# Summing the later modulation vectors over weight blocks on DVE, ACT and POOL in place of thin float32 matmuls

## Chip, core and metric

One core of a Trainium2 chip runs the whole kernel as one program. The metric is the device time of one execution in microseconds; the median of several runs is compared. TensorE does the matmuls, VectorE (DVE), ScalarE (ACT) and GpSimd (POOL) work on tiles in SBUF, and SyncE (SP) issues all the DMAs of this kernel.

## What is computed

Two layers of a diffusion backbone over 512 latent and 256 context tokens, model width 1024. In each layer the tokens are normalised and modulated, go through three groups of attention heads (neighbourhood, latent, differential), are gated, projected and added back. The change concerns the modulation vectors. For each layer and for each of two streams (latent: `c`, context: `c_ctx`) they come from one vector times a 1024 x 3072 matrix:

```python
shift, scale, gate = jnp.split(jax.nn.silu(c) @ w_ada[l] + b_ada[l], 3, axis=-1)
shift_c, scale_c, gate_c = jnp.split(jax.nn.silu(c_ctx) @ w_ada[l] + b_ada[l], 3, axis=-1)
h = rms_norm(x, norm_g[l]) * (1.0 + scale[:, None]) + shift[:, None]
hc = rms_norm(ctx, norm_g[l]) * (1.0 + scale_c) + shift_c
...
x_new = x + gate[:, None] * merge_branches(o_na, o_mla, o_diff, z, gm, w_br[l], w_out[l])
if not last:
    ctx = ctx + gate_c * merge_branches(co_na, co_mla, co_diff, cz, cgm, w_br[l], w_out[l])
```

The last layer needs the gate of the latent stream alone.

## The kernel before, in words

Activations lie transposed in SBUF as pairs of float32r tiles (a high part and what it leaves), so that each product is three matmuls (`mm3`, L115 to L117). Weights come in blocks of 128 x 384 by DMA (`unit`, tile `ws`, L138), ACT makes the high part (`w`, L122), DVE or POOL the low one (L127). A layer is a loop of twelve steps, each with the projection of one head pair (PSUM tiles `pj`, three banks), the attention of the pair before (`sc`, `bk`), a z gate and some gate projections (`zgate`, `gm`, PSUM tile `fl`, one bank); then come the branch projections and `out_proj`, which multiplies by `gate` (L1037).

The order of the instructions on each engine is not the order of the code. A scheduler goes through the program with priorities that the code sets per kind of work (`PRI`, `SHIFT`, `at`), takes what its own time model calls ready, and writes one fixed list per engine. On the chip each engine then takes its list strictly in order and waits where an operand is not there; SP's list of DMAs likewise.

`w_ada` is cut into 6 chunks per layer of 512 columns, each of 8 blocks of 128 x 512 (256 KB). Chunks 0 and 1 are the shift, 2 and 3 the scale, 4 and 5 the gate. The first four chunks of layer 0 are made in the setup (`fast`, tile `fs`) and are not touched. The eight later ones, (0,4), (0,5), all six of layer 1, are made by `ada_later` as background work of low priority (`ada` 2500). There, each block lands in one of four `aw` tiles, and a float32 matmul with the 128 x 32 tile `sT` (two columns of it are the two streams' vectors, the rest zero) adds it into one of four 32-row groups of the bank `fl` (L230). Each such matmul stands in the trace as two records. When eight blocks are in, DVE copies the bank to SBUF (`arow`, L231). For shift and scale, four small matmuls with the selector `C_SEL` (L250) add the row groups and turn the rows into columns, and DVE adds the bias (L254). For the gate, eight rows go to DRAM; `ada_gate` reads them back with the bias as a ninth row (L266, L267), and a matmul with `selb` (L270) sums them and spreads them over 128 partitions.

`rstd` (L166 on DVE, a power on POOL at L167) makes the norms' factors. `mla_prep` makes the latent head group's projections of all tokens at the start of each layer: projection into `pj`, square on ACT, `rstd`, a scaled copy `cn` on DVE, transposes on TensorE (L567), and split copies `ct` which go to DRAM.

Of the kernel before, what the change touches and what calls it, by code (L numbers as in the profile page):

```python
# [7 lines left out]
F32 = mybir.dt.float32  # L8
F32R = mybir.dt.float32r
AF = mybir.ActivationFunctionType  # L10
ALU = mybir.AluOpType
# [3 lines left out]
P = 128  # L15
D = 1024
KT = 8
# [19 lines left out]
C_SEL = 256  # L37
# [15 lines left out]
class Mixer:  # L53
# [114 lines left out]

    # ---------------------------------------------------------------- setup
    def setup(self):  # L170
# [44 lines left out]
    def ada_rows(self, l, ch, rows, pool, fast):  # L215
        nc, io = self.nc, self.io
        ps = self.fl()
        w = io["w_ada"][l, ch]
        for k in range(KT):
            if fast:  # L220
                st = pool.tile([P, 512], F32, tag="fs", bufs=self.FS, name=self.n("fs"))
            else:
                st = self.wpool.tile([P, 512], F32, tag="aw", bufs=4, name=self.n("aw"))
            if self.AFT and not fast:
                with self.tc.issue_after(self.last.ins):
                    nc.sync.dma_start(st, w[:, k])
            else:
                nc.sync.dma_start(st, w[:, k])
            g = 32 * (k % 4)
            nc.tensor.matmul(ps[g:g + 32, :], self.sT[:, k, :], st, start=k < 4, stop=k >= 4, tile_position=(0, g))  # L230
        nc.vector.tensor_copy(rows, ps)  # L231

    def ada_later(self, l, ch, pool):
        rows = pool.tile([P, 512], F32, tag="th", bufs=1, name=self.n("arow"))
        self.ada_rows(l, ch, rows, None, False)
        if ch < 4:
            self.ada_ss(l, ch, rows, self.fl())
            return
        if l not in self.rowsd:
            self.rowsd[l] = self.dram.tile([2, 4, 2, 512], F32, name=f"rowsd{l}")  # L240
        for g in range(4):
            self.nc.sync.dma_start(self.rowsd[l][ch - 4, g], rows[32 * g:32 * g + 2, :])

    def ada_ss(self, l, ch, rows, pt):
        nc = self.nc
        Lp = self.L[l]
        part, hf = ch // 2, ch % 2
        sel = self.cst[:, C_SEL:C_SEL + 2]
        for i in range(4):
            nc.tensor.matmul(pt[:, 2 * i:2 * i + 2], rows[:, i * P:(i + 1) * P], sel, start=True, stop=True)  # L250
        v = pt[:, 0:8].rearrange("p (k s) -> p k s", s=2)
        col = lambda o: Lp["pp"][:, o + 4 * hf:o + 4 * hf + 4].unsqueeze(2).to_broadcast([P, 4, 2])
        d = Lp["AB"[1 - part]][:, 4 * hf:4 * hf + 4, :]
        nc.vector.tensor_tensor(d, v, col(PP_BA + 8 * part), ALU.add)  # L254
        if part == 1:
            nc.vector.scalar_tensor_tensor(d, d, 1.0, col(PP_NG), ALU.add, ALU.mult)

    def ada_gate(self, l, pool):
        nc = self.nc
        strs = (0, 1) if l == 0 else (0,)  # L260
        gate = [pool.tile([P, D], F32, tag=f"gate{s}", bufs=1, name=f"gate{l}_{s}") for s in strs]
        selb = pool.tile([9, 2, P], F32, tag="selb", bufs=1, name=f"selb{l}")
        nc.sync.dma_start(selb, self.io["selb"])
        for hf in range(2):
            rows = pool.tile([9, 512], F32, tag="arow", bufs=1, name=self.n("arow"))
            nc.sync.dma_start(rows[0:8, :], self.rowsd[l][hf].rearrange("g s n -> (g s) n"))  # L266
            nc.sync.dma_start(rows[8:9, :], self.io["b_gate"][l:l + 1, hf * 512:(hf + 1) * 512])  # L267
            for s in strs:
                ps = self.bk()
                nc.tensor.matmul(ps, selb[:, s, :], rows[0:9, :], start=True, stop=True)  # L270
                nc.scalar.mul(gate[s][:, hf * 512:(hf + 1) * 512], ps, 0.25)
        return gate
# [34 lines left out]

    # ---------------------------------------------------------------- h
    def norm_tile(self, pool, xt):
# [66 lines left out]

    # ---------------------------------------------------------------- projections
    def proj_tok(self, ps, ws, t):
# [714 lines left out]
def _consts(np):  # L1093
    c = np.zeros((P, C_N), np.float32)
    c[:, C_ID:C_ID + P] = np.eye(P)
    c[:, C_ONE:C_ONE + P] = 1.0
    selb = np.zeros((9, 2, P), np.float32)
    selb[8] = 1.0
    for s in range(2):
        c[s::32, C_SEL + s] = 1.0  # L1100
        selb[s:8:2, s] = 1.0
    rope = np.zeros((P, S_N), np.float32)
    t = np.arange(SEQ)
    row, col = (t % 8).astype(np.float32), (t // 8).astype(np.float32)
    for co, so, dim in ((S_COSD, S_SIND, 64), (S_COSM, S_SINM, 32)):
# [7 lines left out]
    return c, selb, rope  # L1113


def _layout(np, i):
    a = {k: np.asarray(v) for k, v in i.items()}
    o = {}
    o["cst"], o["selb"], o["rope"] = _consts(np)
    o["x"] = a["x"][0].reshape(8, 64, D).transpose(1, 0, 2).reshape(SEQ, D)  # L1120
# [5 lines left out]
    w = kp(a["w_in"])  # L1126
# [41 lines left out]
```

## Time and profile before

| | |
|---|---|
| runs | 2012.0, 2018.39, 2019.07 us, median 2018.39 |
| profiled execution | span 2015.7 us from first to last instruction; no time beside the span is given for it |
| busy | TensorE 1962.4 us, DVE 1217.9, ACT 938.1, POOL 762.3 |
| granted TensorE clock, mean | 0.990 of full speed |

Span and busy times are of one execution under the hardware profiler. A busy TensorE is not one at its peak, since matmuls overlap and their ends are modelled; idle time before an instruction is put down to the engine or DMA whose signal came last.

### The profile page before, as it was taken

To read this page: it belongs to the slowest core of one execution; us is meant where nothing else is said; L and a number is where in the kernel's file an instruction comes from. 1 tells how busy PE (TensorE), PEld (TensorE's weight loads), DVE (VectorE), ACT (ScalarE), POOL (GpSimd) and SP (SyncE) were. 2 spreads that over 40 slices of the span, in tenths; PEclk is the share of its full clock that TensorE was granted. 3 is DMA by queue.
4 is the path that set the end of the run, shared out by engine and by line. 5 is a ranking of instruction groups with operands and counts; after the bars stand their busy time and mean duration, and the time that the engine had idled before them with its cause. 6 is when DMAs were issued, how large, how long until landed. Compare 5 with 4: busy or idle time off the path is not lost.

```text
span 2015.7 us, 33972 instructions
## 1 busy us (share of the span) xinstructions
PE 1962.4 (97%) x11650; PEld 1745.5 (87%) x11650; DVE 1217.9 (60%) x2808; ACT 938.1 (47%) x2422; POOL 762.3 (38%) x1053
## 2 busy tenths in 40 slices
PE   6999999999999999999999999999999999999998
PEld 4988998998888988989999988897698789889878
DVE  5556667555765555646663465667667466666763
ACT  4445455444544544435532354555455345555531
POOL 3333233323423322332355454334344234343353
PEclk9999999999999999999999999999999899999999
DMA  9553113333434333332655243323513322432663
GB/s 320 185 157 123 41 56 104 110 120 111 124 110 145 90 100 119 98 108 70 199 175 178 92 129 125 110 66 91 163 54 93 112 72 81 119 126 59 189 188 112
DMA packets 172600, 243.28 MB, mean 121 GB/s; under 512 B 22710, under 2 KB 127560, under 8 KB 172428
## 3 DMA queue, kind: packets, MB, share of 16 engines
q1 hardware_dynamic: 172428, 241.12, 38.3%
q8 instruction: 92, 1.51, 0.3%
q14 instruction: 80, 0.66, 0.1%
HBM read 190.38 MB, written 44.49 MB: 117 GB/s over the span
## 4 chain that ended last, share of the span: by engine, by line
PE 90%; DVE 4%; DMA 2%; ACT 1%; issue 1%; POOL 1%; SPq 0%; DVEq 0%; ACTq 0%; POOLq 0%
PE pj L115 11%; PE pj L117 11%; PE pj L116 11%; PE fl L115 10%; PE fl L116 9%; PE fl L117 9%; PE sc L690 9%; PE bk L851 5%; PE bk L680 4%; PE fl L230 2%; PE sc L731 2%; PE bk L810 2%; PE pj L640 1%; PE pj L451 1%; DVE w L127 1%
## 5 line engine op out<-in xcount | busy, mean ns | idle before, releaser
L122 ACT CAST w<-ws 128x384 fp32r<-128x384 f32 (+3 forms) x520 | 237.2, 474 | 268.4 <-PE fl L116 159.2
L127 POOL TENSOR_TENSOR w<-ws,w 128x384 fp32r<-128x384 f32 (+3 forms) x260 | 241.9, 936 | 312.6 <-ACT w L122 301.7
L115 PE MATMUL fl<-h,w 128*128 128x384 f32 (+1 forms) x864 | 316.5, 366 | 4.1 <-DVE zs L392 2.7
L115 PE MATMUL pj<-w,h 128*128 128x384 f32 (+2 forms) x944 | 314.5, 336 | 2.0 <-DVE kl L127 1.1
L117 PE MATMUL fl<-h,w 128*128 128x384 f32 (+1 forms) x864 | 312.8, 362 | 0.0
L116 PE MATMUL fl<-h,w 128*128 128x384 f32 (+1 forms) x864 | 312.8, 362 | 0.0
L116 PE MATMUL pj<-w,h 128*128 128x384 f32 (+2 forms) x944 | 309.6, 330 | 0.0
L117 PE MATMUL pj<-w,h 128*128 128x384 f32 (+2 forms) x944 | 307.5, 330 | 1.0 <-POOL h L127 0.6
L127 DVE TENSOR_TENSOR w<-ws,w 128x384 fp32r<-128x384 f32 (+2 forms) x260 | 177.4, 686 | 74.4 <-ACT w L122 67.0
L167 POOL TENSOR_TENSOR ss<-ss,nhalf 128x4 f32<-128x4 f32 (+1 forms) x144 | 142.8, 992 | 179.2 <-DVE ss L166 166.3
L694 ACT ACTIVATE P<-sc,st 128x768 f32<-128x768 f32 (+1 forms) x192 | 159.5, 832 | 104.7 <-DVE st L796 39.1
L741 POOL TENSOR_SCALAR P<-P,st 128x512 f32<-128x512 f32 (+1 forms) x128 | 107.8, 845 | 256.0 <-DVE st L737 216.7
L684 DVE TENSOR_TENSOR pt<-bk,pt 128x512 fp32r<-128x512 f32 (+1 forms) x256 | 147.8, 586 | 64.9 <-ACT pt L683 62.7
L117 PEld LDWEIGHTS pj<-w,h 128*128 128x128 f32 x944 | 177.0, 189 | 9.6 <-issue 5.9
L115 PEld LDWEIGHTS pj<-w,h 128*128 128x128 f32 x944 | 177.6, 189 | 8.8 <-issue 3.8
L116 PEld LDWEIGHTS pj<-w,h 128*128 128x128 f32 x944 | 178.2, 189 | 5.7 <-issue 5.0
L115 PEld LDWEIGHTS fl<-h,w 128*128 128x128 f32 x864 | 164.4, 190 | 18.3 <-DVE zs L392 4.9
L117 PEld LDWEIGHTS fl<-h,w 128*128 128x128 f32 x864 | 164.1, 190 | 13.1 <-DVE w L127 0.5
L683 ACT CAST pt<-bk 128x512 fp32r<-128x512 f32 (+1 forms) x256 | 126.9, 506 | 104.3 <-PE bk L680 101.8
L116 PEld LDWEIGHTS fl<-h,w 128*128 128x128 f32 x864 | 164.2, 190 | 11.0
L690 PE MATMUL sc<-qk,qk 96*128 96x512 f32 (+3 forms) x592 | 153.2, 353 | 3.0 <-DMA qk<-qk 3.0
L680 PE MATMUL bk<-cst,P 128*128 128x128 f32 x832 | 130.1, 274 | 2.7 <-DVE u L855 1.8
(236 smaller groups left out, 3995.9 us busy)
## 6 DMA issues: line engine op xcount, KB each, us to landing
ws<-in_w_qkv SPq DMA_DIRECT2D x128, 192.0 KB
ws<-in_w_gm SPq DMA_DIRECT2D x96, 192.0 KB
aw<-in_w_ada SPq DMA_DIRECT2D x64, 256.0 KB
ct<-cqd SPq DMA_DIRECT2D x40, 384.0 KB
ct<-ckd SPq DMA_DIRECT2D x48, 256.0 KB
ws<-in_w_z SPq DMA_DIRECT2D x48, 192.0 KB
thd<-th SPq DMA_DIRECT2D x48, 192.0 KB
ws<-in_w_br SPq DMA_DIRECT2D x48, 192.0 KB
```

The source lines that it names most:

```text
L115: mm(out, a[0], b[0], start=first, stop=False)
L116: mm(out, a[0], b[1], start=False, stop=False)
L117: mm(out, a[1], b[0], start=False, stop=last)
L122: nc.scalar.copy(hi, src)
L127: (nc.gpsimd if le == "g" else nc.vector).tensor_tensor(lo, src, f(hi), ALU.subtract)
L167: nc.gpsimd.tensor_tensor(out, out, self.nhalf[:, :cols], ALU.pow)
L680: nc.tensor.transpose(pt[:, i * P:(i + 1) * P], src[:, (b0 + i) * P:(b0 + i + 1) * P], self.ident)
L683: nc.scalar.copy(h, v)
L684: nc.vector.tensor_tensor(lo, v, f(h), ALU.subtract)
L690: mm(s[:, d0:d0 + w], x, y, start=i == 0, stop=i == len(ops) - 1)
L694: nc.scalar.activation(p, src, AF.Exp, bias=st[:, m:m + 1], accum_out=st[:, 2 + m:3 + m])
L741: nc.gpsimd.tensor_scalar(p, p, st[:, 4 + m:5 + m], 0.0, ALU.mult, ALU.add)
```

## The change

`ada_later` no longer uses TensorE for the blocks. Each chunk has an accumulator `acc` of 128 x 512 per stream in SBUF (one buffer). For the first block ACT writes block times the vector's entry of each partition; for the others DVE multiplies and adds for the latent stream, and for the context stream, where it is needed (six of the eight chunks), ACT multiplies the block in place and POOL adds it. What is left to do is a sum over the 128 partitions. For shift and scale, matmuls of `acc` slices with a column of ones do it, one for each stream and slice (eight in place of four). For the gate the whole accumulator goes to DRAM (256 KB per stream in place of 4 KB a row group), is read back by `ada_gate` one stream at a time, DVE adds the bias into its first row, and a matmul with the 128 x 128 ones sums and spreads it. The `aw` tiles are two in place of four.

```diff
     def ada_later(self, l, ch, pool):
-        rows = pool.tile([P, 512], F32, tag="th", bufs=1, name=self.n("arow"))
-        self.ada_rows(l, ch, rows, None, False)
+        nc = self.nc
+        strs = (0, 1) if l == 0 or ch < 4 else (0,)
+        acc = pool.tile([P, 2, 512], F32, tag="acc", bufs=1, name=self.n("acc"))
+        w = self.io["w_ada"][l, ch]
+        for k in range(KT):
+            st = self.wpool.tile([P, 512], F32, tag="aw", bufs=2, name=self.n("aw"))
+            nc.sync.dma_start(st, w[:, k])
+            for s in strs:
+                g = self.sT[:, k, s:s + 1]
+                if k == 0:
+                    nc.scalar.mul(acc[:, s], st, g)
+                elif s == 0:
+                    nc.vector.scalar_tensor_tensor(acc[:, s], st, g, acc[:, s], ALU.mult, ALU.add)
+                else:
+                    nc.scalar.mul(st, st, g)
+                    nc.gpsimd.tensor_tensor(acc[:, s], acc[:, s], st, ALU.add)
         if ch < 4:
-            self.ada_ss(l, ch, rows, self.fl())
+            pt = self.fl()
+            for i in range(4):
+                for s in strs:
+                    nc.tensor.matmul(pt[:, 2 * i + s:2 * i + s + 1], acc[:, s, i * P:(i + 1) * P], self.ones[:, 0:1], start=True, stop=True)
+            self.ada_put(l, ch, pt)
             return
         if l not in self.rowsd:
-            self.rowsd[l] = self.dram.tile([2, 4, 2, 512], F32, name=f"rowsd{l}")
-        for g in range(4):
-            self.nc.sync.dma_start(self.rowsd[l][ch - 4, g], rows[32 * g:32 * g + 2, :])
+            self.rowsd[l] = self.dram.tile([2, 2, P, 512], F32, name=f"rowsd{l}")
+        for s in strs:
+            nc.sync.dma_start(self.rowsd[l][ch - 4, s], acc[:, s])
...
         for hf in range(2):
-            rows = pool.tile([9, 512], F32, tag="arow", bufs=1, name=self.n("arow"))
-            nc.sync.dma_start(rows[0:8, :], self.rowsd[l][hf].rearrange("g s n -> (g s) n"))
-            nc.sync.dma_start(rows[8:9, :], self.io["b_gate"][l:l + 1, hf * 512:(hf + 1) * 512])
+            bias = pool.tile([1, 512], F32, tag="gbias", bufs=1, name=self.n("gbias"))
+            nc.sync.dma_start(bias, self.io["b_gate"][l:l + 1, hf * 512:(hf + 1) * 512])
             for s in strs:
+                rows = pool.tile([P, 512], F32, tag="arow", bufs=1, name=self.n("arow"))
+                nc.sync.dma_start(rows, self.rowsd[l][hf, s])
+                nc.vector.tensor_tensor(rows[0:1, :], rows[0:1, :], bias, ALU.add)
                 ps = self.bk()
-                nc.tensor.matmul(ps, selb[:, s, :], rows[0:9, :], start=True, stop=True)
+                nc.tensor.matmul(ps, self.ones, rows, start=True, stop=True)
                 nc.scalar.mul(gate[s][:, hf * 512:(hf + 1) * 512], ps, 0.25)
```

In the changed kernel most lines of the rest have numbers 17 higher (L680 is L697, L851 is L868); L115 to L167 keep theirs. The blocks' first products are L240, DVE's multiply-adds L242, ACT's products L244, POOL's adds L245.

The scheduler's lists move with it. On TensorE, these rows stood before at the last chunk of `ada_later`, in layer 1, at 1556 to 1566 us of the profile. `pj` is a projection of the latent heads, `fl` with L230 the chunk, `bk` with L680 transposes of probabilities, with L851 attention times V:

```order
L116 MATMUL pj_18796<-w_18787,ct_18797 128x256
L117 MATMUL pj_18796<-w_18786,ct_18797 128x256
L230 MATMUL fl_18512<-aw_18513,sT 32x512
...
L230 MATMUL fl_18512<-aw_18522,sT 32x512
L680 MATMUL bk_18041<-cst,P_18037 128x128 x4
L680 MATMUL bk_18052<-cst,P_18048 128x128 x4
L230 MATMUL fl_18512<-aw_18525,sT 32x512
L851 MATMUL bk_18059<-pt_17987,V_17582 128x256
```

And these stand there now, from the same projection to the same transposes (`fl` with L115 to L117 is a gate projection):

```order
L116 MATMUL pj_18884<-w_18875,ct_18885 128x256
L117 MATMUL pj_18884<-w_18874,ct_18885 128x256
L115 MATMUL fl_19153<-h_0_12883,w_19136 128x512
...
L116 MATMUL fl_19153<-h_1_12884,w_19148 128x512
L697 MATMUL bk_18134<-cst,P_18130 128x128 x4
L697 MATMUL bk_18145<-cst,P_18141 128x128 x4
L117 MATMUL fl_19153<-h_0_12883,w_19149 128x512
```

The chunk is gone from this place (it now lies at the start of the layer), and twenty matmuls of a gate projection, which stood behind it because they need the same bank, have moved ahead of the transposes.

On POOL, this is a piece of the difference at 54 to 69 us, in the context projections of `mla_prep` (`mss` are their norms' powers, `acc` the first chunk's adds for the context stream):

```order
 L167 TENSOR_TENSOR mss_654<-mss_654,nhalf 128x1
+L245 TENSOR_TENSOR acc_5052<-acc_5052,aw_5057 128x512
 L167 TENSOR_TENSOR mss_698<-mss_698,nhalf 128x1
+L245 TENSOR_TENSOR acc_5052<-acc_5052,aw_5062 128x512
+L245 TENSOR_TENSOR acc_5052<-acc_5052,aw_5067 128x512
 L167 TENSOR_TENSOR mss_742<-mss_742,nhalf 128x1
 L127 TENSOR_TENSOR w_815<-ws_811,w_814 128x384
```

The adds have come in between the powers; in the first 165 us there are 21 of them.

On DVE, these rows now stand in `mla_prep` of layer 1, from 1188 us of the profile before (`aw` numbers name the blocks of one chunk in turn; `cn`, `mss` and `ct` belong to the projections of the context and latent tokens):

```order
L242 SCALAR_TENSOR_TENSOR acc_17311<-aw_17321,sT,acc_17311 128x512
L576 TENSOR_SCALAR cn_14120<-pj_14095,mss_14121 128x384
L242 SCALAR_TENSOR_TENSOR acc_17311<-aw_17324,sT,acc_17311 128x512
L242 SCALAR_TENSOR_TENSOR acc_17311<-aw_17327,sT,acc_17311 128x512
L166 TENSOR_SCALAR mss_14160<-mss_14160 128x1
L588 TENSOR_TENSOR ct_14043<-bk_14040,ct_14043 128x256
L242 SCALAR_TENSOR_TENSOR acc_17311<-aw_17330,sT,acc_17311 128x512
L576 TENSOR_SCALAR cn_14159<-pj_14134,mss_14160 128x384
```

Before, none of the L242 rows were there; the chunk ran at 1439 to 1450 us on TensorE. Block 17327 takes the buffer of block 17321, two blocks before it.

## Rows read from the trace of the kernel before

**Rows 1.** The page: span; busy by engine; GB/s by slice; the ending chain.

```profile
span 2015.7 us, 33972 instructions
...
PE 1962.4 (97%) x11650; PEld 1745.5 (87%) x11650; DVE 1217.9 (60%) x2808; ACT 938.1 (47%) x2422; POOL 762.3 (38%) x1053
...
GB/s 320 185 157 123 41 56 104 110 120 111 124 110 145 90 100 119 98 108 70 199 175 178 92 129 125 110 66 91 163 54 93 112 72 81 119 126 59 189 188 112
...
PE 90%; DVE 4%; DMA 2%; ACT 1%; issue 1%; POOL 1%; SPq 0%; DVEq 0%; ACTq 0%; POOLq 0%
PE pj L115 11%; PE pj L117 11%; PE pj L116 11%; PE fl L115 10%; PE fl L116 9%; PE fl L117 9%; PE sc L690 9%; PE bk L851 5%; PE bk L680 4%; PE fl L230 2%; PE sc L731 2%; PE bk L810 2%; PE pj L640 1%; PE pj L451 1%; DVE w L127 1%
```

**Rows 2.** Timeline of TensorE, first chunk: start, length (us), instructions.

```profile
439.54 1.06 PE L230 MATMUL fl<-aw,sT 128*32 128x512 f32 x8
...
448.05 0.34 PE L116 MATMUL pj<-w,h 128*128 128x384 f32 x1
448.32 1.05 PE L230 MATMUL fl<-aw,sT 128*32 128x512 f32 x4
449.30 0.44 PE L117 MATMUL pj<-w,h 128*128 128x384 f32 x1
```

**Rows 3.** Groups by line and shape, whole span: busy, mean ns, idle before.

```profile
L230 PE MATMUL fl<-aw,sT 128*32 128x512 f32 x128 | 39.2, 626 | 4.6 <-DMA aw<-in_w_ada 3.7 <-ACT th L990 0.9
```

**Rows 4.** Timeline of TensorE in the last chunk, and a window with its clock.

```profile
1563.34 1.05 PE L230 MATMUL fl<-aw,sT 128*32 128x512 f32 x2 [3.70 <-DMA aw<-in_w_ada]
...
1567.02 1.92 PE L230 MATMUL fl<-aw,sT 128*32 128x512 f32 x2
...
1577.67 0.63 PE L115 MATMUL fl<-h,w 128*128 128x512 f32 x1
...
1564.00:1582.00 18.00, 18.00 (x55) 11.83 (x55) 3.94 (x9) 2.93 (x8) 0.92 (x2) 0.53 0.12 40
```

**Rows 5.** Groups by line: L250 from 600 to 1000 us, L270 whole span.

```profile
L250 PE MATMUL fl<-cst,arow 128*128 128x2 f32 x32 | 3.8, 240 | 0.0
...
L270 PE MATMUL bk<-arow,selb 9*128 9x512 f32 x12 | 6.5, 631 | 1.2 <-DMA arow<-rowsd 1.2
```

**Rows 6.** Timeline at the end: the last gate rows.

```profile
1963.01 0.29 SPq L266 DMA_DIRECT2D arow<-rowsd  x1
...
1969.46 1.12 PE L270 MATMUL bk<-arow,selb 9*128 9x512 f32 x2 [1.22 <-DMA arow<-rowsd]
```

**Rows 7.** Groups by line and shape: instructions near to the added ones.

```profile
L801 DVE SCALAR_TENSOR_TENSOR P<-P,st,P 128x768 f32<-128x768 f32 x32 | 32.6, 1019 | 0.1
L978 POOL TENSOR_TENSOR yf<-yf,tht 128x512 f32<-128x512 f32 x16 | 23.7, 1488 | 6.6 <-DVE tht L977 6.5
...
L990 ACT ACTIVATE th<-fl 128x512 f32<-128x512 f32 x24 | 14.3, 596 | 0.1
```

**Rows 8.** Timeline, first chunk: blocks issued on SP and awaited by TensorE.

```profile
440.61 1.76 SPq L228 DMA_DIRECT2D aw<-in_w_ada  x4
...
444.53 0.14 PEld L230 LDWEIGHTS fl<-aw,sT 128*32 128x32 f32 x2 [0.21 <-DMA aw<-in_w_ada]
```

**Rows 9.** Windows: busy PE, PEld, DVE, ACT, POOL; clock; DMA share; GB/s.

```profile
50.00:100.00 50.00, 48.72 (x305) 48.18 (x304) 26.63 (x70) 20.79 (x68) 17.80 (x21) 0.98 0.56 184
100.00:150.00 50.00, 47.19 (x278) 44.59 (x277) 28.73 (x75) 21.82 (x66) 19.04 (x27) 1.00 0.54 162
...
640.00:665.00 25.00, 25.00 (x150) 19.98 (x149) 15.24 (x37) 10.92 (x27) 6.74 (x8) 1.00 0.33 104
...
1150.00:1200.00 50.00, 46.84 (x309) 43.55 (x308) 30.75 (x81) 26.84 (x82) 29.42 (x43) 1.00 0.44 140
1200.00:1250.00 50.00, 47.19 (x257) 41.56 (x257) 29.81 (x76) 22.08 (x62) 22.43 (x29) 0.97 0.42 132
```

**Rows 10.** Instructions of L127 by engine: ns min/median/max, first and last start.

```profile
L127 POOL TENSOR_TENSOR w<-ws,w x260: 453/1010/1384, 35.3 to 1995.9; 128x384 fp32r<-128x384 f32 x80, 128x128 fp32r<-128x128 f32 x24, 128x256 fp32r<-128x256 f32 x22, 128x288 fp32r<-128x288 f32 x4
...
L127 DVE TENSOR_TENSOR w<-ws,w x260: 405/558/1389, 28.3 to 1994.0; 128x384 fp32r<-128x384 f32 x104, 128x256 fp32r<-128x256 f32 x22, 128x288 fp32r<-128x288 f32 x4
```

More of the change, by code (lines that the diff above doesn't have):

```diff
@@ L222, in ada_rows @@
             else:
[L223 to L228, printed above, removed]
+                raise AssertionError
+            nc.sync.dma_start(st, w[:, k])
             g = 32 * (k % 4)
@@ L233, in ada_later, with ada_put @@
     def ada_later(self, l, ch, pool):
-        rows = pool.tile([P, 512], F32, tag="th", bufs=1, name=self.n("arow"))
-        self.ada_rows(l, ch, rows, None, False)
-        if ch < 4:
-            self.ada_ss(l, ch, rows, self.fl())
+        nc = self.nc
[4 more added lines that the diff above has]
+            st = self.wpool.tile([P, 512], F32, tag="aw", bufs=2, name=self.n("aw"))
+            nc.sync.dma_start(st, w[:, k])
+            for s in strs:
[7 more added lines that the diff above has]
+                    nc.gpsimd.tensor_tensor(acc[:, s], acc[:, s], st, ALU.add)
+        if ch < 4:
+            pt = self.fl()
[3 more added lines that the diff above has]
+            self.ada_put(l, ch, pt)
             return
         if l not in self.rowsd:
-            self.rowsd[l] = self.dram.tile([2, 4, 2, 512], F32, name=f"rowsd{l}")
-        for g in range(4):
-            self.nc.sync.dma_start(self.rowsd[l][ch - 4, g], rows[32 * g:32 * g + 2, :])
+            self.rowsd[l] = self.dram.tile([2, 2, P, 512], F32, name=f"rowsd{l}")
+        for s in strs:
+            nc.sync.dma_start(self.rowsd[l][ch - 4, s], acc[:, s])
     def ada_ss(self, l, ch, rows, pt):
+        sel = self.cst[:, C_SEL:C_SEL + 2]
+        for i in range(4):
+            self.nc.tensor.matmul(pt[:, 2 * i:2 * i + 2], rows[:, i * P:(i + 1) * P], sel, start=True, stop=True)
+        self.ada_put(l, ch, pt)
+    def ada_put(self, l, ch, pt):
         nc = self.nc
@@ L247, in ada_ss @@
         part, hf = ch // 2, ch % 2
-        sel = self.cst[:, C_SEL:C_SEL + 2]
-        for i in range(4):
-            nc.tensor.matmul(pt[:, 2 * i:2 * i + 2], rows[:, i * P:(i + 1) * P], sel, start=True, stop=True)
         v = pt[:, 0:8].rearrange("p (k s) -> p k s", s=2)
@@ L1096, in _consts @@
     c[:, C_ONE:C_ONE + P] = 1.0
-    selb = np.zeros((9, 2, P), np.float32)
-    selb[8] = 1.0
     for s in range(2):
         c[s::32, C_SEL + s] = 1.0
-        selb[s:8:2, s] = 1.0
     rope = np.zeros((P, S_N), np.float32)
@@ L1112, in _consts @@
             rope[:, off:off + 4 * dim] = full.reshape(P, 4 * dim)
-    return c, selb, rope
+    return c, rope
 def _layout(np, i):
@@ L1118, in _layout @@
     o = {}
-    o["cst"], o["selb"], o["rope"] = _consts(np)
+    o["cst"], o["rope"] = _consts(np)
     o["x"] = a["x"][0].reshape(8, 64, D).transpose(1, 0, 2).reshape(SEQ, D)
```

2 lines of the change are left out of this document (removed).

## The prediction, made blind

> **What bounds the kernel now.** I read the page first: the busy time by engine and the chain of work that ended last [rows 1]. TensorE is busy 1962.4 of 2015.7 us, and 90% of the chain is PE; the float32 matmuls of the later modulation vectors (L230) alone hold 2% of it, about 40 us. DVE, ACT and POOL are busy 60, 47 and 38%. So time taken out of TensorE's stream counts almost in full, and work put on the others costs nothing as long as TensorE is not made to wait for it.
>
> Then the timeline of TensorE around one chunk of L230 [rows 2]. The reader is to see that a burst of these matmuls holds the engine about 1.05 us whether it has 8 records or 4 (each matmul is two records, and four column groups run side by side): behind the L116 at 448.05 the next L117 starts 1.25 us later, where the same stream otherwise goes on inside the 0.34 us that one of them lasts. The group of L230 by line [rows 3] gives the sum over all bursts: 128 records, 39.2 us of occupied time (their mean of 626 ns counts overlapping records twice, so it must not be multiplied), and 4.6 us of idle time just ahead of them, 3.7 of it one wait for a block of w_ada.
>
> Last, that one wait, in the timeline and the windows [rows 4]. TensorE stood for 3.70 us ahead of 1563.34, and from 1564 to 1582 the granted clock was 0.53, nearly all at the lower level (1.2 GHz), where a burst of L230 took 1.92 us in place of 1.05.
>
> **The change, term by term.** All terms are against the profiled execution, whose span is 2015.7 us; no time outside the span is given for it. It lies 2.7 us under the median of the three runs (2018.39) and inside them (2012.0 to 2019.07).
>
> *Removed from TensorE.* All 64 matmuls of L230 on aw go: -39.2 and the idle time ahead of them, -4.6 [rows 3], together -43.8 us. The lower clock goes with its cause: 18 us x (1 - 0.53) = 8.5 us lost, of which 2 x (1.92 - 1.05) = 1.7 already stands in the 39.2, so -6.7 [rows 4]. The order bears this out: where TensorE stood at 1559, the bank fl is no longer held by L230, and the gate projections on fl that ran from 1577.7 are now issued there.
>
> *Added to TensorE.* The partition sum for four chunks takes 8 one-column matmuls on the ones in place of 4 on the selector. The 32 records of the four chunks now take 3.8 us [rows 5]; twice as many take twice that: +3.8. The gate matmuls keep their number and their 512 columns, with 128 rows in place of 9. No row here shows a 128x128 by 512 float32 matmul in one column group; the nearest, L230 (128 rows) and L270 (9 rows), have means of 626 and 631 ns a record [rows 3, 5], so I take 0; were each record to last as long as the slowest burst of L230, 1.92 us for two, 12 records would cost 4 us more.
>
> *The gate rows at the end.* Before, the last arow transfer (8 x 512 float32, 16 KB) was issued at 1963.01, behind loads of xn (128 x 1024, 512 KB each), and TensorE waited 1.22 us for it until 1969.46 [rows 6]. It now moves 256 KB. With the DMA at 112 to 189 GB/s in the last three slices [rows 1], 240 KB more take 1.3 to 2.1 us, and the added bias sum on DVE stands behind it, which I take at the 0.68 us of a 512-column DVE instruction (below). So this wait grows by 2 to 2.8 us. Bounds: 0, if the gate's place in the order hides it; 2.8 + 6.7 = 9.5, if the longer stop also brings the low clock for as long as the stop of 3.70 us did. I take +4, nearer the low end because the wait stays under 3.7 or just at it.
>
> *Added to DVE, ACT and POOL.* Eight chunks, eight blocks each. DVE: 7 scalar_tensor_tensor per chunk, 56; the nearest row is L801, 1019 ns for 768 columns, so 0.68 us for 512 by columns, 38 us; 8 copies out of PSUM go. ACT: 14 first blocks and 42 scaled blocks, 56 x 0.60 (L990, 128x512) = 34 us. POOL: 42 adds x 1.49 (L978, 128x512) = 63 us [rows 7]. That brings them to about 62, 48 and 41% of the span, far from bounding it. What covers them is TensorE's own full stream; what they can cost is order: each engine takes its instructions in order, so a multiply that waits for a block of w_ada holds the PSUM evictions and norms behind it, and an add on POOL holds the powers (L167) that the norms need.
>
> By the times at which their neighbours in the order ran before, the chunks now lie in five clusters: three chunks (two clusters) before 165 us, one near 650, two between 745 and 790, and both of layer 1 in that layer's first 32 us, 1182 to 1214. With two buffers for the blocks in place of four, each transfer waits until the block two before it is used up. A block issued at 440.61 was still awaited at 444.53 in the profile [rows 8], so up to 3.9 us for one, with others in flight. In the rows of DVE in layer 1 that are shown above, block 17327's multiply stands one multiply and one norm behind the one that frees its buffer: DVE will stand there for a microsecond or two, with mss and ct of the context projections queued behind it, and TensorE's transposes wait for those.
>
> How much of it reaches TensorE no row shows. From below: nothing, since the pj banks and the full stream can ride over it. From above: one stop like the 3.70 us one in each of the eight chunks, with its clock: 8 x (3.7 + 6.7) = 83 us. The rows nearest to the clusters are the stretches themselves [rows 9]: TensorE now idles 1.3, 2.8, 0.0, 3.2 and 2.8 us in them. I take as much again, 10 us, and 1.5 for one more short clock drop (1200 to 1250 has 0.97 of 50 us): +12, close to the low end, because such waits do not add up: once TensorE is late by one, the next finds its operand there.
>
> **Sum:** 2015.7 - 43.8 - 6.7 + 3.8 + 4 + 12 = 1985.0. With both unknowns at nothing it is 1969; without the clusters' term alone 1973.
>
> **Rivals.** *A, slower: the two-buffer wait starves TensorE.* In each chunk one multiply waits at the head of ACT or DVE, the evictions behind it come late, all pj banks fill, and TensorE stops for as long as it did at 1559. Each stop costs 3.7 + 6.7 = 10.4 us, so the 42.7 us that the rest of the change gives (2015.7 - 1973) are gone at 4.1 stops; eight give 1973 + 83 = 2056. For it: the clusters at 45 to 165 and 1182 to 1214 lie in stretches that idle now, with the DMA at 0.56 and 0.44. Against: over the whole profile TensorE idles only 53 us, whoever it waits for [rows 1].
>
> *B, near the old time: POOL's queue holds the norms.* In the first cluster 21 adds stand among the powers of the context projections, two or three in a row, as the piece of POOL's order shows. If each shows in full on TensorE, 21 x 1.49 = 31 us: 1973 + 31 = 2004. DVE and POOL also slow each other when both read SBUF tensors: L127 on DVE lasts 558 ns at the median and 1389 at worst, on POOL 1010 and 1384 [rows 10]. If each of the 21 multiplies loses that 0.83 too, 17 us more: 2021. I put this case at 2004 to 2021. Against: POOL is idle three fifths of these stretches, and TensorE has other projections to run. A sentence of the Trainium skill speaks for it and against the change: SBUF — State Buffer, section "Who interferes with whom", says that a DVE instruction with two SBUF inputs and a GpSimd instruction that reads SBUF shut each other out for the whole length of the first. The trace agrees in kind, by the spread in [rows 10]. By that rule alone, each of the 56 multiplies could stand for up to the add's whole 1.49 us, 83 us of DVE's idle time in all; none of it need reach TensorE, so the sum would stay, and what would is this rival.
>
> *C, a larger gain.* The bank fl was held through each chunk (10 us in the chunk at 439) and is now free for the gate projections, so waits elsewhere shrink as well. With the clusters' term at nothing and a third of the remaining 49 us of idle time gone, 1969 - 16 = 1953.
>
> That TensorE's time does not come back at all is excluded: nothing else runs in those 43.8 us.
>
> **How the numbers follow.** Forecast (1965 to 2004) 0.64; C (below 1965) 0.10; B (2004 to 2021) 0.16; A 0.10. The range leaves out the deeper half of C and nearly all of A: 1960 to 2016. What a measurement of this kernel can tell from no change is about 0.5%, 10 us: faster means under 2008. That takes the forecast, C and a third of B: 0.79. Same: 0.11, the rest of B. Slower: 0.10, A.
>
> **What would show it.** PE's busy time should fall to about 1927 (1962.4 - 39.2 + 3.8); L230 should be left with its 64 records of the setup; TensorE's idle time should come out near 58 to 65 us, as much as before. The half-clock stretch at 1564 should be gone. If A is right, the waits of PE name DVE or ACT in the five clusters with stops over 2 us, followed by granted clocks near 0.5. If B is right, POOL's powers start late behind L245 in the first 165 us and idle time of PE there is above 20 us. The forecast fails if idle time in the clusters rises by more than 35 us in all.

## The result, and the profile after

The changed kernel takes 2064.05 us (median of 4 runs, 2060.0 to 2065.52), the kernel before 2015.77 (4 runs): a ratio of 1.0233, 95% interval 1.0209 to 1.0257. It is slower by 48 us where 31 us faster was forecast, and it lies outside the range.

The page of the changed kernel: span, busy time by engine, and the chain that ended last, by engine and by line.

```profile
span 2063.4 us, 33924 instructions
...
PE 1960.4 (95%) x11554; PEld 1770.0 (86%) x11554; DVE 1265.2 (61%) x2862; ACT 972.9 (47%) x2478; POOL 823.1 (40%) x1095
...
PE 80%; DVE 7%; DMA 4%; ACT 4%; issue 2%; POOL 2%; SPq 0%; ACTq 0%; DVEq 0%; POOLq 0%
PE pj L115 9%; PE fl L115 9%; PE pj L116 9%; PE pj L117 9%; PE fl L116 9%; PE fl L117 9%; PE sc L707 8%; PE bk L868 5%; PE bk L697 4%; DMA aw<-in_w_ada 3%; PE sc L748 2%; PE bk L827 2%; DVE acc L242 1%; PE pj L657 1%; DVE w L127 1%
```

Against [rows 1]: L230 is gone from the chain, yet TensorE's busy time fell by only 2.0 us, not by 35: most of what went is made up for by some 29 us more of low clock (2063.4 x 0.024 - 2015.7 x 0.010), at which a matmul is busy for longer [rows 4]. The time in which it is not busy rose from 53.3 us (2015.7 - 1962.4) to 103.0, and its share of the chain fell from 90 to 80%. DVE, DMA and ACT took that share, by name `DMA aw<-in_w_ada` and `DVE acc L242`, the new work.

The new instructions, as groups of the changed kernel by line and shape: busy, mean ns, idle time ahead of them and who ended it.

```profile
L245 POOL TENSOR_TENSOR acc<-acc,aw 128x512 f32<-128x512 f32 x42 | 57.6, 1372 | 44.7 <-ACT aw L244 44.3
L242 DVE SCALAR_TENSOR_TENSOR acc<-aw,sT,acc 128x512 f32<-128x512 f32 x56 | 53.4, 954 | 39.5 <-DMA aw<-in_w_ada 34.3 <-ACT acc L240 3.4 <-ACT w L122 1.8
L244 ACT ACTIVATE aw<-aw,sT 128x512 f32<-128x512 f32 x42 | 30.4, 724 | 35.9 <-DVE acc L242 26.6 <-DVE mss L166 4.0 <-issue 2.1
L240 ACT ACTIVATE acc<-aw,sT 128x512 f32<-128x512 f32 x14 | 9.5, 719 | 9.0 <-PE fl L250 8.5 <-DVE ct L588 0.4 <-DMA rowsd<-acc 0.2
...
L250 PE MATMUL fl<-cst,acc 128*128 128x1 f32 x64 | 7.5, 245 | 1.3 <-DVE acc L242 1.3
L287 PE MATMUL bk<-arow,cst 128*128 128x512 f32 x12 | 6.2, 600 | 0.0
L261 PE MATMUL fl<-cst,arow 128*128 128x2 f32 x32 | 4.1, 250 | 2.6 <-DVE arow L227 2.6
```

The idle column is to be read as a chain. DVE stands 34.3 us for blocks that have not landed. The in-place product on ACT stands 26.6 us for DVE, which must have read the block first. POOL stands 44.3 us for that product, and only POOL's add frees the buffer for the next transfer. While an instruction stands so, everything behind it on its engine stands too.

The stretches of the clusters, as windows of the changed kernel (columns as in [rows 9]).

```profile
50.00:100.00 50.00, 44.97 (x277) 42.82 (x276) 30.67 (x71) 24.99 (x72) 24.63 (x25) 0.98 0.58 185
100.00:150.00 50.00, 39.81 (x198) 38.45 (x198) 34.91 (x68) 23.60 (x58) 31.91 (x31) 0.84 0.57 181
650.00:700.00 50.00, 45.34 (x277) 43.07 (x276) 29.35 (x66) 25.08 (x55) 23.67 (x22) 0.93 0.23 72
...
800.00:850.00 50.00, 43.58 (x227) 39.60 (x226) 28.80 (x60) 24.50 (x61) 21.12 (x22) 0.93 0.39 121
1250.00:1300.00 50.00, 41.13 (x199) 36.45 (x198) 31.47 (x71) 17.86 (x53) 18.63 (x24) 0.86 0.44 136
```

From 100 to 150 us TensorE idled 2.8 us before [rows 9]; now it idles 10.2, and does 198 matmuls in place of 278. The clock is the second loss: 0.84 of full speed there, after stops of 3 to 4 us, and 0.976 over the span, where 0.99 was granted before.

Two of the stops, in the timeline of the changed kernel: start, length (us), engine, line, instruction, idle before and its releaser.

```profile
669.75 1.28 POOL L245 TENSOR_TENSOR acc<-acc,aw 128x512 f32<-128x512 f32 x1
669.89 0.38 PE L697 MATMUL bk<-cst,P 128*128 128x128 f32 x2
670.04 1.54 DVE L242 SCALAR_TENSOR_TENSOR acc<-aw,sT,acc 128x512 f32<-128x512 f32 x1 [1.22 <-DMA aw<-in_w_ada]
671.62 0.69 DVE L701 TENSOR_TENSOR pt<-bk,pt 128x512 fp32r<-128x512 f32 x1
671.67 0.72 ACT L244 ACTIVATE aw<-aw,sT 128x512 f32<-128x512 f32 x1 [1.53 <-DVE acc L242]
...
672.36 0.66 PE L697 MATMUL bk<-cst,P 128*128 128x128 f32 x4 [2.08 <-DVE pt L701]
...
812.83 1.41 POOL L245 TENSOR_TENSOR acc<-acc,aw 128x512 f32<-128x512 f32 x1
813.04 1.48 DVE L460 TENSOR_TENSOR qn<-qn,t 128x256 f32<-128x256 f32 x1
...
815.34 1.44 POOL L245 TENSOR_TENSOR acc<-acc,aw 128x512 f32<-128x512 f32 x1
815.58 1.48 DVE L462 TENSOR_TENSOR qn<-qn,ss 128x256 f32<-128x256 f32 x1
817.20 0.66 PE L468 MATMUL pj<-cst,qn 128*128 128x128 f32 x2 [4.57 <-DVE qn L462]
```

In the first, a multiply stands 1.22 us at the head of DVE's queue for its block, then takes 1.54 us in place of 0.75 beside POOL's add; the eviction of the transposed P (L701) runs behind it, ACT's product waits for it, and TensorE, whose bank bk that eviction frees, stands 2.08 us. In the second no block is late: two steps of q's norm take 1.48 us in place of some 0.42, each while POOL's add runs; TensorE stands 4.57 us, of which the two steps' excess is 2.1. A multiply waiting for its block is rival A's mechanism, DVE and POOL slowing each other is one half of rival B's.

### The profile page after: what moved, and what is told of

The parts are those of the page before. It is cut to its first block, busy times and chain, and to the rows that moved or that the text cites. A ratio compares the mean times of both kernels' runs of the same rounds, so it can differ in the third digit from the quotient of the medians.

```text
span 2063.4 us, 33924 instructions
## 1 busy us (share of the span) xinstructions
PE 1960.4 (95%) x11554; PEld 1770.0 (86%) x11554; DVE 1265.2 (61%) x2862; ACT 972.9 (47%) x2478; POOL 823.1 (40%) x1095
## 3 DMA queue, kind: packets, MB, share of 16 engines
q8 instruction: 91, 1.49, 0.3%
## 4 chain that ended last, share of the span: by engine, by line
PE 80%; DVE 7%; DMA 4%; ACT 4%; issue 2%; POOL 2%; SPq 0%; ACTq 0%; DVEq 0%; POOLq 0%
PE pj L115 9%; PE fl L115 9%; PE pj L116 9%; PE pj L117 9%; PE fl L116 9%; PE fl L117 9%; PE sc L707 8%; PE bk L868 5%; PE bk L697 4%; DMA aw<-in_w_ada 3%; PE sc L748 2%; PE bk L827 2%; DVE acc L242 1%; PE pj L657 1%; DVE w L127 1%
## 5 line engine op out<-in xcount | busy, mean ns | idle before, releaser
L127 POOL TENSOR_TENSOR w<-ws,w 128x384 fp32r<-128x384 f32 (+3 forms) x260 | 248.5, 962 | 329.6 <-ACT w L122 312.7
L115 PE MATMUL fl<-h,w 128*128 128x384 f32 (+1 forms) x864 | 321.0, 372 | 11.9 <-DVE zs L409 7.0
L115 PE MATMUL pj<-w,h 128*128 128x384 f32 (+2 forms) x944 | 319.6, 342 | 3.3 <-ACT w L122 1.5
L116 PE MATMUL pj<-w,h 128*128 128x384 f32 (+2 forms) x944 | 314.5, 335 | 5.0 <-DVE w L127 3.9
L117 PE MATMUL fl<-h,w 128*128 128x384 f32 (+1 forms) x864 | 315.8, 365 | 1.0 <-DVE w L127 1.0
L116 PE MATMUL fl<-h,w 128*128 128x384 f32 (+1 forms) x864 | 315.1, 365 | 0.0
L117 PE MATMUL pj<-w,h 128*128 128x384 f32 (+2 forms) x944 | 312.8, 335 | 1.0 <-POOL h L127 0.6
L127 DVE TENSOR_TENSOR w<-ws,w 128x384 fp32r<-128x384 f32 (+2 forms) x260 | 173.3, 670 | 81.1 <-ACT w L122 76.2
L167 POOL TENSOR_TENSOR ss<-ss,nhalf 128x4 f32<-128x4 f32 (+1 forms) x144 | 143.9, 1000 | 175.5 <-DVE ss L166 160.0
L115 PEld LDWEIGHTS fl<-h,w 128*128 128x128 f32 x864 | 166.4, 193 | 29.7 <-DVE zs L409 9.9
L701 DVE TENSOR_TENSOR pt<-bk,pt 128x512 fp32r<-128x512 f32 (+1 forms) x256 | 147.8, 586 | 68.7 <-ACT pt L700 65.5
L115 PEld LDWEIGHTS pj<-w,h 128*128 128x128 f32 x944 | 181.9, 194 | 9.0 <-ACT w L122 3.0
L116 PEld LDWEIGHTS pj<-w,h 128*128 128x128 f32 x944 | 182.5, 194 | 7.2 <-DVE w L127 4.7
L117 PEld LDWEIGHTS pj<-w,h 128*128 128x128 f32 x944 | 181.2, 193 | 5.4 <-DVE h L363 2.3
L117 PEld LDWEIGHTS fl<-h,w 128*128 128x128 f32 x864 | 166.3, 192 | 15.7 <-DVE w L127 2.6
L116 PEld LDWEIGHTS fl<-h,w 128*128 128x128 f32 x864 | 166.6, 193 | 10.7
L697 PE MATMUL bk<-cst,P 128*128 128x128 f32 x832 | 129.5, 275 | 12.3 <-DVE pt L701 7.8
```

The costliest lines, as they stand in the source:

```text
L115: mm(out, a[0], b[0], start=first, stop=False)
L116: mm(out, a[0], b[1], start=False, stop=False)
L117: mm(out, a[1], b[0], start=False, stop=last)
L127: (nc.gpsimd if le == "g" else nc.vector).tensor_tensor(lo, src, f(hi), ALU.subtract)
L167: nc.gpsimd.tensor_tensor(out, out, self.nhalf[:, :cols], ALU.pow)
L697: nc.tensor.transpose(pt[:, i * P:(i + 1) * P], src[:, (b0 + i) * P:(b0 + i + 1) * P], self.ident)
```

## The experiments

The theories. **One**: the transfers, two buffers deep, starve TensorE (rival A). **Two**: the work itself, in queues that run in order, delays norms and evictions, block landed or not (B). **Three**: the removal was worth less than its price, so the forecast was too low even with nothing added. The expectation of e10_none numbers them otherwise: its theory 1 is two here, its theory 2 is three. A fourth, that of the place, is that chunks cost because they now lie inside the context projections. "Not busy" below is span less PE's busy time; the clock is its mean. Times and ratios are against the kernel before on the same chip (2014 to 2016 us). Each edit also moves the scheduler's lists, so a run's cost is that of its edit together with the order that came of it. Five runs came out in no theory's range: e1_aw4, e7_late, e8_late4, e11_dve1 and f7_same.

| kernel | us | ratio, 95% interval | PE busy | not busy | clock | PE busy, 50 to 165 us |
|---|---|---|---|---|---|---|
| before | 2015.8 | 1 | 1962.4 | 53.3 | 0.990 | 110.9 |
| after | 2064.1 | 1.0233 (1.0209, 1.0257) | 1960.4 | 103.0 | 0.976 | 98.8 |
| e10_none | 2000.8 | 0.9935 (0.9919, 0.9952) | 1933.3 | 69.1 | 0.987 | 110.5 |
| e11_dve1 | 2021.2 | 1.0030 (1.0009, 1.0050) | 1942.8 | 76.4 | 0.983 | 110.4 |
| e2_nodma | 2036.1 | 1.0103 (1.0081, 1.0124) | 1941.7 | 90.8 | 0.982 | 99.1 |
| e3_noctx | 2037.3 | 1.0097 (1.0071, 1.0123) | 1946.6 | 88.6 | 0.980 | 100.5 |
| e1_aw4 | 2043.5 | 1.0139 (1.0120, 1.0159) | 1952.5 | 93.2 | 0.977 | 96.7 |
| e5_dve | 2052.7 | 1.0196 (1.0177, 1.0214) | 1958.0 | 96.5 | 0.971 | 97.8 |
| e7_late | 2023.2 | 1.0041 (1.0028, 1.0054) | 1942.3 | 79.2 | 0.983 | 110.2 |
| e8_late4 | 2038.9 | 1.0126 (1.0110, 1.0143) | 1949.0 | 88.7 | 0.979 | 109.8 |
| e12_late_dve | 2028.9 | 1.0072 (1.0057, 1.0087) | 1948.2 | 76.8 | 0.979 | 110.6 |
| f3_quad | 1998.3 | 0.9923 (0.9906, 0.9939) | 1936.5 | 59.1 | 0.993 | 110.9 |
| f4_half | 1999.1 | 0.9928 (0.9912, 0.9944) | 1934.1 | 62.4 | 0.991 | 111.0 |
| f7_same | 2034.7 | 1.0101 (1.0082, 1.0120) | 1974.6 | 55.0 | 0.994 | 110.2 |

### Four corners: transfers and the context stream

e2_nodma, without transfers:

```diff
-            st = self.wpool.tile([P, 512], F32, tag="aw", bufs=2, name=self.n("aw"))
-            nc.sync.dma_start(st, w[:, k])
+            if not hasattr(self, "awc"):
+                self.awc = [self.wpool.tile([P, 512], F32, tag=f"awc{i}", bufs=1, name=f"awc{i}") for i in range(2)]
+                for i in range(2):
+                    nc.sync.dma_start(self.awc[i], w[:, i])
+            st = self.awc[k % 2]
```

> The change without the block transfers: two tiles are loaded once and all multiplies read these, so the modulation vectors of the later chunks are made of the same two blocks. All work on DVE, ACT and POOL stays in the same places. The theory of the transfers expects the loss gone and the gain on TensorE left: 1970 to 1990 us. The theory of the work itself expects 2045 to 2065. The place theory gives no waits of its own without transfers beyond those of the work: 2000 to 2040.

e3_noctx, without the second stream's products on ACT and adds on POOL:

```diff
-            for s in strs:
+            for s in (0,):
                 g = self.sT[:, k, s:s + 1]
...
-            nc.sync.dma_start(self.rowsd[l][ch - 4, s], acc[:, s])
+            nc.sync.dma_start(self.rowsd[l][ch - 4, s], acc[:, 0])
```

> The change without the context stream in the blocks: no products on ACT (42) and no adds on POOL (42); the sums of the latent stream stand for both streams. DVE's 56 multiplies and all transfers with two buffers stay. The theory of the transfers expects the waits of DVE to stay, a little shorter since a buffer is free two engines earlier: 2015 to 2045 us. The theory of the work itself expects the loss gone with POOL's 42 adds and ACT's 42 products: 1975 to 2000.

e11_dve1 has both edits:

> The changed kernel without block transfers (two tiles loaded once) and without the work on blocks for the context stream: of the work on blocks only VectorE's 56 sums of 0.75 us are left. With the runs without transfers (2036 us) and without the context stream (2037 us) it makes the fourth corner. If transfers and context stream cost apart from each other: 2064 - 28 - 27 = about 2009 us, and VectorE's sums alone cost some 8 us over the run without work on blocks (2001 us). If either alone is enough to hold the queues: 2030 to 2036 us.

e10_none does no work on blocks beyond the first product:

```diff
         for k in range(KT):
+            if k:
+                continue
...
```

> The changed kernel with all work on blocks left out: of each chunk only the first ScalarE product stays, from one tile that is loaded once; the small matmuls of the norms, the rows of the gate and their order stay (so the modulation vectors lack 7 of 8 blocks). Theory 1 (the work on blocks in the in-order queues costs the time, and the removal was priced right): TensorE's busy time falls by the 39.2 us of L230, the idle time is that of the kernel before, and the time is 1965 to 1980 us. Theory 2 (the order that is left when the thin matmuls are gone has gaps of its own, since the thin matmuls had filled time in which TensorE would wait anyway): stops outside the old clusters and low clock stay, the time is 1985 to 2005 us, and the removal is worth 10 to 30 us in place of 44.

Measured, from the bottom: 2000.8 with no work on blocks; 2021.2 with DVE's 56 sums alone (+20); 2036.1 when ACT's products and POOL's adds join them (+15), 2037.3 when the transfers do (+16); 2064.1 with both (+27 or +28 on either). So no cause alone explains the loss: each removed by itself gives back 27 us and leaves the kernel slower than before. The last column shows how they combine in the first two clusters. Transfers alone and the context stream alone each bring TensorE from 110.4 us of work down to 100.5 or 99.1 of 115, and both together to 98.8: either one holds the queues there, and taking away one alone frees little.

Over the rest of the kernel it is the other way about. Lateness is read here from when TensorE has done the same number of matmul records, those of the modulation left out (11382 remain in every kernel). After 165 us e2_nodma and e3_noctx fall 16 and 21 us further behind e10_none, about what e11_dve1 does with DVE's sums alone (19); the changed kernel falls 40 behind. There the loss beyond the sums needs transfers and context stream together. That is why each of them adds only 15 or 16 us by itself, and its removal gives back 27. Of the 19 for the sums alone, 7 come between 640 and 800 us and 8 between 950 and 1000 us, where TensorE stands 3.42 us for a round trip described below (`uT`); by which multiplies is not shown.

What the context stream does to DVE stands in the rows of the sums, first e11_dve1, then e2_nodma; neither has transfers.

```profile
L245 DVE SCALAR_TENSOR_TENSOR acc<-awc,sT,acc 128x512 f32<-128x512 f32 x56 | 43.1, 770 | 6.3 <-ACT acc L243 5.8
```

```profile
L245 DVE SCALAR_TENSOR_TENSOR acc<-awc,sT,acc 128x512 f32<-128x512 f32 x56 | 55.7, 995 | 11.5 <-ACT acc L243 9.8 <-DVE acc L245 0.5 <-ACT awc L247 0.5
```

With POOL's adds beside them the same 56 multiplies take 995 ns in the mean in place of 770: 12.6 us in all. That is in line with the rule of the Trainium skill that the prediction named (SBUF — State Buffer, "Who interferes with whom"): the trace agrees, and it agrees too in the 1.48 us norms above.

### Buffers, engine and place

e1_aw4 has `bufs=4` for the blocks in place of 2:

> The change with four buffers for the blocks of w_ada in place of two; nothing else. The theory of the transfers (an instruction at the head of DVE or ACT waits for a block whose transfer could not start before a buffer came free, and what is queued behind it comes late) expects most of these waits to shrink, since a transfer is now issued two blocks earlier: 2015 to 2035 us against 2064 of the change, and the 34 us that DVE waits for blocks at least halved. The theory of the work itself (in-order chain DVE, ACT, POOL of each block holds the norms) expects no gain: 2055 to 2070. The theory of the place (chunks inside the context projections) expects little: 2045 to 2065.

e5_dve sums both streams on DVE:

```diff
-                elif s == 0:
+                else:
                     nc.vector.scalar_tensor_tensor(acc[:, s], st, g, acc[:, s], ALU.mult, ALU.add)
-                else:
-                    nc.scalar.mul(st, st, g)
-                    nc.gpsimd.tensor_tensor(acc[:, s], acc[:, s], st, ALU.add)
```

> The changed kernel with the sums of both streams made by VectorE (ScalarE makes only the first products, GpSimd adds nothing); two buffers and the early place stay. A buffer is then free when VectorE has read it, and no ScalarE product waits for VectorE, no GpSimd add for ScalarE; VectorE has 42 more instructions of 0.75 us, 31 us. If the chain from ScalarE through GpSimd to the buffer is what costs (about 27 us by the run without the context stream): 2035 to 2045 us. If the waits of VectorE for the transfers are what costs: 2050 to 2068 us.

e7_late holds the block transfers back, which moves DVE's multiplies to 379 to 449, 573 to 596, 683 to 851, 1413 to 1426 and 1518 to 1531 us:

```diff
-            nc.sync.dma_start(st, w[:, k])
+            with self.tc.issue_after(self.last.ins):
+                nc.sync.dma_start(st, w[:, k])
```

> The change with each block's transfer issued only after the last weight transfer of its step, which moves the chunks out of the context projections to where the order had them before: 370 to 440, 565 to 585, 680 to 835, 1400 and 1505 us. Two buffers and all the work stay. The theory of the place expects the loss to fall by most: 1985 to 2015 us. The theory of the transfers expects as many waits elsewhere: 2040 to 2070, and so does the theory of the work itself.

e8_late4 is e7_late with four buffers, e12_late_dve is e7_late with both streams on DVE:

> The changed kernel with late block transfers (issued only after the last instruction before them, as in the kernel before) and four block buffers in place of two. If place and buffers cure different waits the gains add: 2064 - 41 - 21 = about 2002 us, faster than the kernel before. If both cure the same wait (VectorE and ScalarE held in their queues by a block that has not landed), four buffers add little to the late place: 2018 to 2024 us.

> The changed kernel with late block transfers and with both streams summed by VectorE, two buffers; its output is the full computation. If place (41 us) and the chain from ScalarE to GpSimd (11 us) add: about 2012 us, even with the kernel before. If the order that the scheduler then finds decides, as with four buffers: 2023 to 2040 us.

(An aside in the first of these is wrong: the kernel before has such a switch, but it is off there.)

Four buffers save 21 us and cut DVE's wait for transfers from 34.3 to 6.6 us, yet not in the first clusters, where TensorE does 96.7 us of work; DVE for both streams saves 11. The place saves 41, the most of any single edit: in the stretch of the first two clusters TensorE is back at 110.2 of 115 us, and over the span the stops above 2 us fall from ten (31 us) to four (10 us). But DVE still waits 29.0 us for blocks, so here the place of these waits weighs more than their length. The gains do not add: late with four buffers is 16 us slower than late with two, late with DVE 6 us slower. In e8_late4 the largest wait of TensorE is for the evictions of the z projection (in total, times, longest; 10.0, 10, 2.3 in e7_late), and its longest stop is one of them (columns as in the timeline above):

```profile
PE fl L115 <- DVE zs L410: 12.5, 11, 5.0
```

```profile
689.00 0.72 ACT L245 ACTIVATE aw<-aw,sT 128x512 f32<-128x512 f32 x1
...
689.92 0.48 ACT L409 ACTIVATE zs<-fl 128x384 f32<-128x384 f32 x1
...
691.32 1.39 DVE L243 SCALAR_TENSOR_TENSOR acc<-aw,sT,acc 128x512 f32<-128x512 f32 x1 [1.23 <-DMA aw<-in_w_ada]
...
692.63 0.54 DVE L410 SCALAR_TENSOR_TENSOR zs<-zs,fl 128x384 f32<-128x384 f32 x1
...
693.23 0.69 PE L115 MATMUL fl<-h,w 128*128 128x384 f32 x1 [4.95 <-DVE zs L410]
```

Here ACT has products (L245) ahead of its half of the eviction (L409), and on DVE a multiply stands 1.23 us for its block and runs 1.39 ahead of the other half (L410). So with four buffers too a late block can hold TensorE. That a deeper prefetch makes the late place worse is measured; why, over the whole span, stays open.

### What the removal was worth

f3_quad is the kernel before with four blocks in one transfer, so that four thin matmuls stand ready together:

```diff
         for k in range(KT):
+            if not fast:
+                if k % 4 == 0:
+                    quad = self.wpool.tile([P, 4, 512], F32, tag="aw", bufs=1, name=self.n("aw"))
+                    nc.sync.dma_start(quad, w[:, k:k + 4])
+                st = quad[:, k % 4]
...
             g = 32 * (k % 4)
             nc.tensor.matmul(ps[g:g + 32, :], self.sT[:, k, :], st, start=k < 4, stop=k >= 4, tile_position=(0, g))
```

> The kernel before with one transfer for four blocks into one tile, in place of four transfers into four tiles, so that the thin matmuls stand ready four at a time. If the 39.2 us of L230 is mostly the single matmul with its load (some 1.15 us each) that stands alone among other work: bursts of four overlap their loads and the time falls by 5 to 20 us (1995 to 2010 us). If the order of the rest or the longer transfer decides: 2010 to 2025 us.

f7_same is f3_quad with all blocks in one column group:

```diff
-            g = 32 * (k % 4)
-            nc.tensor.matmul(ps[g:g + 32, :], self.sT[:, k, :], st, start=k < 4, stop=k >= 4, tile_position=(0, g))
+            g = 32 * (k % 4) if fast else 0
+            first, last = (k < 4, k >= 4) if fast else (k == 0, k == KT - 1)
+            nc.tensor.matmul(ps[g:g + 32, :], self.sT[:, k, :], st, start=first, stop=last, tile_position=(0, g))
...
```

> The kernel before with one transfer for four blocks, as in the run of 1998 us, but all eight blocks of a chunk are summed in the same 32 columns of the array and the same 32 rows of PSUM (the other rows are set to zero by VectorE). If four thin matmuls cost 1.06 us because they lie in four column groups and run side by side: L230 is back at about 38 us of busy time and the time at 2010 to 2020 us. If the burst is cheap because the blocks stand ready together, without loads and gaps between: L230 stays near 18 us and the time near 1998 us.

f4_half is f3_quad with only the first four blocks of each chunk (`range(KT if fast else 4)`):

> The kernel before with one transfer of four blocks per chunk and the other four blocks left out (the modulation vectors lack half of their blocks), so 8 bursts of four thin matmuls stand in place of 64 single ones; no work goes to other engines. If taking the thin matmuls away is worth its price wherever the order of the rest stays: 2014 - 44 + 8 x 1.06 = about 1980 us, and the 24 us that the run without work on blocks gave back come from the place that the scheduler gives the chunks there. If the thin matmuls had filled time in which TensorE would wait anyway: the time stays at 1992 to 2002 us, near the run with sixteen bursts (1998 us) and the run without work on blocks (2001 us).

The group of the thin matmuls and one burst in the timeline, of f3_quad and then of f7_same.

```profile
L230 PE MATMUL fl<-aw,sT 128*32 128x512 f32 x128 | 17.9, 633 | 4.0 <-DMA aw<-in_w_ada 4.0
...
440.66 1.06 PE L230 MATMUL fl<-aw,sT 128*32 128x512 f32 x8
```

```profile
L231 PE MATMUL fl<-aw,sT 128*32 128x512 f32 x128 | 58.3, 596 | 2.6 <-DMA aw<-in_w_ada 2.6
...
443.40 3.62 PE L231 MATMUL fl<-aw,sT 128*32 128x512 f32 x8
```

Four thin matmuls in four column groups take 1.06 us, in one group 3.62: they run side by side. The Trainium skill (TensorEngine Tiling (Array Packing), "Theoretical Speedup") gives up to 4x where the small dimension is at most 32; these rows, with 32 output columns, give 3.4. In the kernel before they came in bursts of four, two and one [rows 2, 4], 39.2 us in all [rows 3]; in bursts of four they take 17.9, and the kernel takes 1998.3 us. It computes the whole result and beats both kernels, with no work moved. Down to there TensorE's time counts nearly in full: f7_same has 40.4 us more of thin matmuls than f3_quad and takes 36 longer, 19.1 more than the kernel before and takes 20 longer; f3_quad has 21.3 less than the kernel before and takes 16 less.

f4_half then takes out half of the rest, 8.3 us of busy time, and gains nothing: 1999.1. With e10_none at 2000.8 that makes three kernels, with 17.9, 9.6 and 0 us of this work on TensorE, that agree within 3 us. At about 2000 us something else sets the time. One place of it shows in f4_half's chain of waits from 930 to 1000 us (start, length, what):

```profile
943.74 0.69 ACT P L694 x2
944.48 0.37 PE sc L731
944.85 4.67 DMA uraw<-ud
949.54 0.84 ACT uT L122
950.43 0.69 PE fl L115
...
981.04 2.92 DMA uraw<-ud
...
987.09 4.69 DMA uraw<-ud
```

The attention's outputs go to DRAM and come back (ud, uraw) before they are projected. TensorE, some 20 us ahead of its old times at 900 us (counted by matmul records, as above), waits for that round trip; 13 us of low clock follow the stop of 3.36 us that ends at 950, and at 1000 us it is 10 us ahead. In the kernel before no such transfer stands in the chain there. f3_quad and e10_none, 14 and 13 us ahead at 900 us, are 10 us ahead at 1000 too, so the three come out of this stage level. In e10_none another round trip stands in the chain there, that of the gate's accumulator (`arow<-rowsd`, 4.39 us at 995.65), so they need not share one limit. In e10_none the waits of TensorE on other work grew (in total, times, longest):

```profile
PE fl L115 <- DVE zs L413: 8.7, 6, 3.3
...
PE sc L752 <- ACT P L715: 3.6, 4, 1.8
PE fl L115 <- ACT th L1011: 3.1, 4, 1.2
```

Before these were 2.7, 0.8 and 0.6 us, so these three grew by 11.3 us, where its time not busy grew by 15.8 in all (other waits rose and fell).

## Why the prediction was wrong, by its own steps

**Removed from TensorE: right in size, wrong in worth.** L230 went from TensorE, with nothing of it left in the trace but the setup's 64 records. But the step "time taken out of TensorE's stream counts almost in full" failed. Removal with the ones matmuls was to give 43.8 + 6.7 - 3.8 = 46.7 us; e10_none gave 13.4 (2014.3 to 2000.8). TensorE's busy time fell by 29.1 there, which is about the 39.2 less 3.6 for the ones matmuls and 6 for more low clock (2002.4 x 0.013 against 2015.7 x 0.010), and the time not busy rose by 15.8. The two claims behind it fell: that TensorE at 97% busy is bound by itself alone, and that the low clock goes with its cause (it is gone from that place in the changed kernel, but in e10_none 10 us of it stand at 1559 again, behind other waits). The sentence "nothing else runs in those 43.8 us" did not help: TensorE came sooner to operands that were not ready sooner, as seen above for the round trip and for the waits of e10_none. Time taken off counts until the kernel reaches some 2000 us and no further: 21.3 us off gave 16 in f3_quad, 8.3 more gave nothing in f4_half. Both keep the chunks near their old places, so it is not the new place of the chunks.

**The clusters' waits: the step that failed most.** The term was +12 us, in bounds of 0 to 83. From e10_none to the changed kernel it is 2064.1 - 2000.8 = 63. The ground given for the low end, that such waits do not add up, was wrong across clusters: behind e10_none the changed kernel is 21 us late at 165 us, 50 at 800 and 66 at 1300. The lower clock that follows the stops was priced once (1.5 us) where the span has about 23 us more of it than e10_none (2063.4 x 0.024 - 2002.4 x 0.013). In the first two clusters the two causes do overlap, later they make each other worse, as the four corners show. The prediction's own sign says the same: TensorE's idle time came out at 103 us, where 58 to 65 were named.

**Rival A was the sign, not the whole.** It gave 2056 by eight stops; ten stops over 2 us stand in the trace, 31 us in all, eight of them in or beside the clusters, with low clocks behind them. But without any transfer the kernel is still 1% slower than before, and that 2056 lies near the result is luck: its base of 1973 is 28 us under e10_none, and its 83 us stand against 63. **Rival B** (2004 to 2021) was right in part. DVE and POOL do slow each other: ten multiplies and three norm steps last over 1 us beside an add. That the powers come late behind the adds is rare: in the first 165 us two start over 2 us after their operand directly behind an add (at 107.6 and 126.9 us). Its price of 31 to 48 us is above the 15 that the context stream costs without transfers and the 27 with them (and its bound of 83 us of idle time counts 56 adds where there are 42); its time came out too low because the base was. A and B together are what happened; I had priced them as alternatives.

**The small terms were nearly right.** Ones matmuls: 7.5 + 4.1 - 8.0 = +3.6 (forecast +3.8). Gate matmuls: 6.2 against 6.5 us (0). The gate rows at the end: TensorE does not wait for them any more (L287 has no idle time ahead), so 0, the lower bound, for +4. Durations: 0.75 us at the median for the multiplies (0.68), 0.72 for ACT (0.60), 1.29 for POOL's adds (1.49).

The two large misses, 46.7 - 13.4 = 33 and 63 - 12 = 51, less the 4 of the gate rows, are the 80 us or so between forecast and result.

## What to carry to other kernels

A busy share of 97% does not say that what is taken off the engine comes back: here what was put on it counted nearly in full, and what was taken off only down to the next limit. So before counting it in full, take the work out, which is one run, and see what the rest does. Work moved to engines that idle half the time still costs when it waits at the head of an in-order queue: ask what stands behind it, whether its operand can be late, and how many engines one buffer passes through before it is free. And before moving thin matmuls elsewhere, see whether they can run side by side where they are.

## What was not expected of the hardware

Where a DVE instruction with two SBUF operands meets POOL's add, it is stretched by almost the whole add: 1.48 us for 256 columns in place of 0.42, and multiplies of up to 1.78 us with a median of 0.75. In the kernel before the worst of these norm steps took 1.24, beside POOL's low parts of weights (L127). ACT's 128x512 product took 0.72 us from SBUF to SBUF, where L990, which reads PSUM, took 0.60 [rows 7]. The two differ in source, in function and in scale (a column of `sT` against the constant 0.5), and no run here tells which of these makes the difference.
